# One dense block's gate matrix added up in DRAM by scattered adds instead of being built by matmuls

## The chip, the cores and the metric

The kernel runs on one core of one Trainium2 chip. The metric is the device time of one execution in microseconds (us). TensorE multiplies matrices, VectorE (DVE) and ScalarE (ACT) do elementwise work, GpSimd (POOL) does some of that and issues the DMAs whose addresses are data, SyncE (SP) issues most plain DMAs. Each engine works through its own list of instructions in order.

## The reference

One encoder layer over 512 tokens of width 1024: a mixer (two branches and a projection), then PEER, a product-key mixture of 128 x 128 single-neuron experts, and a final norm. The change touches PEER alone:

```python
def block(xb):                                  # 128 tokens at a time
    qh = (xb @ w_q).reshape(T, 8, 2, 128)       # 8 heads, 2 halves
    s = jnp.einsum('thpc,hpnc->thpn', qh, sk)   # against 128 sub-keys
    s1, i1 = lax.top_k(s[:, :, 0], 16); s2, i2 = lax.top_k(s[:, :, 1], 16)
    # the 16 best of the 256 sums s1 + s2; their experts are i1 * 128 + i2
    g = softmax(top_s)
    u = u_tab[experts]; v = v_tab[experts]
    act = gelu(einsum('td,thkd->thk', xb, u)) * g
    return einsum('thk,thkd->td', act, v)
```

So each token uses 8 x 16 = 128 (expert, gate) pairs. Two heads can choose the same expert; their gates then add up.

## The kernel before, in words

The mixer comes first (`hyena`, then `hgrn`, eight heads, each with five projections of the weights `w_in`). A projection is 24 matmuls of 512 columns: fp32 is split into a high and a low half, and three products are added up. Its weights come through `wraw` (3 buffers), issued on SP in the order of use. ACT makes the high half (`whi`), DVE the low half (`wlo`).

PEER cuts the tokens into four blocks of 128. Block 0 (`GTB`) is gathered: for each of its 128 choices one indirect DMA on POOL's queue fetches 128 rows of `u` or `v` (`grow`), and DVE does the dot products and sums. Blocks 1 to 3 (`DTB`) are dense. The experts are taken as 128 "rows" of 128. For one row, `act_row` multiplies its `u` by the 384 tokens (24 matmuls of 384 columns, `ps_a`), ACT applies gelu (`gact`), and two rows make a pair. `gated` multiplies a pair by the gates, `combine` multiplies by the row's `v` (18 matmuls of 512 columns into `acc`).

The gates for that stand in `Gd` in DRAM, expert by token. `gates_out` makes them for one block in 32 iterations of 4 tokens: DVE compares indices (`one`) and multiplies by the gates (`own`), ACT copies (`rows`), PE does four fp32 matmuls, each two instructions in the trace (`ps_g`), ACT copies the result (`Gs`), SP stores it.

The order of the work is this.
- `queries`: 16 score units `hp` (a projection by `w_q`, four small matmuls, then `top16` on DVE for each of the four blocks: five instructions over 128 scores). From `hp` 8 on, one step of `select` is run beside each. `select` turns the scores of four heads (a "part") into experts `eid` and gates; parts 0 of blocks 1 and 2 are done here (`EARLY`).
- `main`: the other four parts and `gates_out` of the three blocks. `weave` sets an `act_row` beside every `PER` of the costs that they yield. `2 * KEPT + RING - LEFT` = 27 rows are done before the loop; the rows of `KEPT` = 7 pairs go to DRAM, the others wait in a ring in SBUF. The low halves of these rows (`ul`) are DVE's.
- The loop `rows` over the 128 rows, with the rest of `act_row`, `gated`, `split_v` (load `vraw`, halves `vh` on ACT and `vl` on DVE) and `combine`. `gathered` is woven in, 2.25 steps a row: the two parts of block 0's `select`, 7 steps each, then 256 gathers. In the loop `ul` is POOL's, in its queue among the gathers.

An instruction stands in its engine's list where a scheduler puts it; SP's list is in order too, so a load that waits holds up all loads behind it. Pools are stacked: the space of a closed pool goes to the next one, whose first writer then waits for the last user.

## Time and profile before

| | before |
|---|---|
| three runs | 2130.71, 2137.34, 2142.05 us (median 2137.34) |
| profiled execution, time | 2140.67 us |
| profiled execution, span from the first to the last instruction | 2138.9 us |
| first `top16` / first matmul into `acc` / last one starts | 820.5 / 1175.1 / 2130.8 us |

The busy time of an engine is its share of the span, and matmul ends are modelled, so the distance from one matmul's start to the next is a better price than its duration. The granted clock is TensorE's, 1.00 being the higher of its two levels.

### The profile page before, as it was taken

Reading aid. Unit: us, or ns where it says so; the run is one execution under the profiler, and the core shown is the slowest. Engines: PE = TensorE matmul, PEld = TensorE weight load, DVE = VectorE, ACT = ScalarE, POOL = GpSimd, SP = SyncE. Lnnn points to the kernel's source line nnn. Section 1 sums busy time; section 2 is a strip of 40 time slices with the busy share of each in tenths; the row PEclk is TensorE's granted clock in tenths of the full one; section 3 lists DMA queues with packets and bytes.
Section 4 is the critical chain, followed back from the end, with each engine's and each line's share of the span. In section 5 each row is a group of like instructions: output and inputs, shape, how many; then the busy total and the mean of one; then the engine's idle time right before and its main releaser. Section 6 shows DMA issues by size and latency. Waiting matters only on the chain.

```text
span 2138.9 us, 29773 instructions
## 1 busy us (share of the span) xinstructions
PE 2061.9 (96%) x11109; PEld 1819.3 (85%) x11109; DVE 1697.0 (79%) x3073; ACT 962.4 (45%) x1382; POOL 617.1 (29%) x361
## 2 busy tenths in 40 slices
PE   7999999999999999989989999999999999999998
PEld 6888888888888898778889888899888888899987
DVE  6788765999997648999999787787777668778765
ACT  5555435666565623337776332332332323332333
POOL 0000000000000000000001566777776666677640
PEclk9999999999999999989999999999999999999999
DMA  6212222221222434124547988888898888889964
GB/s 194 82 50 65 70 69 100 62 70 60 70 63 75 137 130 139 50 72 173 202 161 245 312 287 299 309 325 309 285 324 281 301 303 313 306 292 333 316 217 158
DMA packets 153661, 406.89 MB, mean 190 GB/s; under 512 B 12425, under 2 KB 65419, under 8 KB 151852
## 3 DMA queue, kind: packets, MB, share of 16 engines
q1 hardware_dynamic: 109884, 255.59, 35.5%
q0 software_dynamic: 36864, 134.23, 17.2%
q10 hardware_dynamic: 6768, 15.17, 2.0%
q8 instruction: 87, 1.43, 0.3%
q14 instruction: 58, 0.48, 0.1%
HBM read 372.83 MB, written 32.11 MB: 189 GB/s over the span
## 4 chain that ended last, share of the span: by engine, by line
PE 56%; DVE 20%; DMA 9%; issue 7%; ACT 4%; POOL 3%; DVEq 0%; ACTq 0%; POOLq 0%; SPq 0%
PE ps_mm L97 7%; PE ps_mm L95 7%; PE ps_mm L94 7%; PE acc L973 5%; PE acc L974 4%; PE acc L972 4%; PE ps_a L94 4%; PE ps_a L97 4%; PE ps_a L95 4%; DMA grow<-in_u,gidx 3%; DMA vraw<-in_v 3%; DMA grow<-in_v,gidx 2%; PE ps_g L1228 2%; POOL grow L904 2%; PE ps_x L718 2%
## 5 line engine op out<-in xcount | busy, mean ns | idle before, releaser
L86 POOL TENSOR_TENSOR ul<-uraw,uh 128x1024 fp32r<-128x1024 f32 x100 | 257.6, 2576 | 634.2 <-DMA uraw<-in_uT 396.4
L85 ACT CAST vh<-vraw 128x1024 fp32r<-128x1024 f32 x128 | 134.7, 1053 | 597.5 <-DMA vraw<-in_v 525.0
L94 PE MATMUL ps_a<-pxh,uh 128*128 128x384 f32 x1008 | 343.9, 341 | 23.6 <-ACT gact L865 23.4
L95 PE MATMUL ps_a<-pxl,uh 128*128 128x384 f32 x1008 | 342.3, 340 | 0.0
L973 PE MATMUL acc<-vl,gh 128*128 128x512 f32 x768 | 300.7, 392 | 0.4 <-DVE vl L86 0.4
L974 PE MATMUL acc<-vh,gl 128*128 128x512 f32 x768 | 300.8, 392 | 0.0
L972 PE MATMUL acc<-vh,gh 128*128 128x512 f32 x768 | 298.8, 389 | 0.0
L933 DVE SCALAR_TENSOR_TENSOR xg<-grow,gw,xg 128x1024 f32<-128x1024 f32 x127 | 194.9, 1534 | 88.6 <-DMA grow<-in_v,gidx 87.5
L94 PE MATMUL ps_mm<-xh,whi 128*128 128x512 f32 (+1 forms) x656 | 259.4, 397 | 1.6 <-ACT xh L195 1.3
L924 DVE SCALAR_TENSOR_TENSOR grow<-grow,xg 128x1024 f32<-128x1024 f32 x128 | 189.4, 1497 | 88.5 <-DMA grow<-in_u,gidx 88.5
L95 PE MATMUL ps_mm<-xl,whi 128*128 128x512 f32 (+1 forms) x656 | 255.2, 390 | 0.3 <-DVE xl L196 0.3
L94 PEld LDWEIGHTS ps_a<-pxh,uh 128*128 128x128 f32 x1008 | 191.1, 190 | 34.1 <-ACT gact L865 30.8
L826 POOL IOTA iota<- 128x512 bf16 x1 | 1.2, 1237 | 756.5 <-DVE gt L281 756.5
L97 PE MATMUL ps_a<-pxh,ul 128*128 128x384 f32 x1008 | 200.9, 340 | 10.7 <-DVE ul L86 10.3
L86 DVE TENSOR_TENSOR vl<-vraw,vh 128x1024 fp32r<-128x1024 f32 x128 | 188.9, 1477 | 18.9 <-ACT vh L85 18.8
L904 POOL DMA_INDIRECT grow<-in_u,gidx x128 | 185.8, 1451 | 45.3 <-issue 22.4
L95 PEld LDWEIGHTS ps_a<-pxl,uh 128*128 128x128 f32 x1008 | 191.1, 190 | 3.2
L97 PEld LDWEIGHTS ps_a<-pxh,ul 128*128 128x128 f32 x1008 | 177.7, 190 | 12.9 <-DVE ul L86 12.3
L904 POOL DMA_INDIRECT grow<-in_v,gidx x128 | 172.3, 1346 | 34.8 <-issue 18.6
L85 ACT CAST whi<-wraw 128x1024 fp32r<-128x1024 f32 x112 | 117.3, 1050 | 133.1 <-PE ps_mm L95 122.6
L974 PEld LDWEIGHTS acc<-vh,gl 128*128 128x128 f32 x768 | 144.1, 188 | 30.2
L973 PEld LDWEIGHTS acc<-vl,gh 128*128 128x128 f32 x768 | 144.1, 188 | 28.9 <-DVE vl L86 0.8
(413 smaller groups left out, 4150.3 us busy)
## 6 DMA issues: line engine op xcount, KB each, us to landing
uraw<-in_uT SPq DMA_DIRECT2D x128, 512.0 KB, 6.9
vraw<-in_v SPq DMA_DIRECT2D x128, 512.0 KB, 5.5
wraw<-in_w_in SPq DMA_DIRECT2D x80, 512.0 KB, 3.6
Gd<-Gs SPq DMA_DIRECT2D x12, 2048.0 KB, 7.3
gt<-Gd SPq DMA_DIRECT2D x32, 768.0 KB, 9.4
wraw<-in_w_q SPq DMA_DIRECT2D x16, 512.0 KB, 4.3
wraw<-in_w_b SPq DMA_DIRECT2D x8, 512.0 KB, 3.6
wraw<-in_w_a SPq DMA_DIRECT2D x8, 512.0 KB, 4.3
```

The source lines that it names most:

```text
L85: nc.scalar.copy(hi, src)
L86: return (eng or nc.vector).tensor_sub(lo, src, hi).ins
L94: nc.tensor.matmul(out, ah, bh, start=(i == 0), stop=False)
L95: nc.tensor.matmul(out, *((al, bh) if late else (ah, bl)), start=False, stop=False)
L97: nc.tensor.matmul(out, *((ah, bl) if late else (al, bh)), start=False, stop=(stop and i == n - 1))
L718: nc.tensor.matmul(pl[:, cs], KM[:, 0, cs], KM[:, 1, cs], start=True, stop=True)
L904: nc.gpsimd.indirect_dma_start(out=t, out_offset=None, in_=tab, in_offset=bass.IndirectOffsetOnAxis(ap=gidx[:, j : j + 1], axis=0))
L924: nc.vector.scalar_tensor_tensor(t, t, 1.0, xg, op0=ALU.mult, op1=ALU.mult, accum_out=gdot[:, j : j + 1])
L933: nc.vector.scalar_tensor_tensor(gacc, t, gw[:, j : j + 1], gacc, op0=ALU.mult, op1=ALU.add)
L972: nc.tensor.matmul(acc[k][:, c], gh[:, ts_], vh[:, ds_], start=(r == 0), stop=False)
L973: nc.tensor.matmul(acc[k][:, c], gh[:, ts_], vl[:, ds_], start=False, stop=False)
L974: nc.tensor.matmul(acc[k][:, c], gl[:, ts_], vh[:, ds_], start=False, stop=(r == NK - 1))
```

## The change

Block 1 (`SCT`) no longer goes through `gates_out`. A DRAM array `Gx` of 128 x 128 x 128 floats is filled with zeros during the mixer (16 stores of 512 KB). As soon as a part of block 1 is selected, `add_gates` computes the places (expert x 128 + token) and issues 64 indirect DMAs on POOL's queue, one for each choice: each adds 128 floats, one a token, to 128 places. The 16 adds of a head wait for all 16 of the head before, since heads may share an expert. `gated` loads the gates of block 1 from `Gx` and of blocks 2 and 3 (`MTB`) from `Gd`, and multiplies twice.

Beside it: `KEPT` 13 for 7 and `RING` 14 for 16, so 37 rows stand ahead of the loop; an `act_row` beside each `hp` from 8 on, and two steps of `select`; the scores of block 0 are kept (`s0`), and its `top16` calls are put into `gathered`; `vraw` has three buffers; parts ahead of the gates count 1.3 times in `weave`.

```diff
-        C.Gd = dp.tile([12, P, P * 32], F32, name="Gd")
+        C.Gd = dp.tile([NG, P, P * GQ], F32, name="Gd")
+        C.Gx = {tb: dp.tile([P * P * P, 1], F32, name=f"Gx{tb}") for tb in SCT}
...
+        zero = mp.tile([P, 1024], F32, name="zero")
+        nc.vector.memset(zero, 0.0)
+        C.zeros = {tb: [] for tb in SCT}
+        for tb, gx in C.Gx.items():
+            dst = gx.rearrange("(p c x) o -> p c (x o)", p=P, x=1024)
+            for c in range(P * P // 1024):
+                C.zeros[tb].append(nc.sync.dma_start(dst[:, c], zero).ins)
...
+SCT = (1,)
+MTB = (2, 3)
 ND = len(DTB) * P
+NX = len(SCT) * P
 T0 = DTB[0] * P
-RING = 16
-KEPT = 7
+RING = 14
+KEPT = 13
+FIRSTC = 1.3
 LEFT = 3
 ...
 MIX = 3
-STEPS = 1
+STEPS = 2
 LAG = 4
 GQ = 32
-NG = ND // GQ
+NG = len(MTB) * P // GQ
...
+    row = cp.tile([P, 1], F32, name="row")
+    nc.gpsimd.iota(row, pattern=[[1, 1]], base=0, channel_multiplier=1, allow_small_or_imprecise_dtypes=True)
+    place = {tb: cp.tile([P, P], I32, name=f"place{tb}") for tb in SCT}
+    added = {}
+    def add_gates(tb, part):
+        n = HEADS // 2 * TOPK
+        ks = slice(part * n, part * n + n)
+        nc.vector.tensor_scalar(place[tb][:, ks], eid[:, tb, ks], float(P), row, op0=ALU.mult, op1=ALU.add)
+        for hd in range(part * HEADS // 2, (part + 1) * HEADS // 2):
+            ins = []
+            for j in range(hd * TOPK, hd * TOPK + TOPK):
+                i = nc.gpsimd.indirect_dma_start(out=C.Gx[tb], out_offset=bass.IndirectOffsetOnAxis(ap=place[tb][:, j : j + 1], axis=0),
+                                                 in_=gate[:, tb, j : j + 1], in_offset=None, compute_op=ALU.add).ins
+                tc.declare_no_dep(i, group=f"add{tb}.{hd}", reason="the experts of one head differ")
+                tc.add_to_no_dep_group(f"add{tb}.{hd}", i)
+                behind(i, added[tb, hd - 1] if hd else C.zeros[tb])
+                ins.append(i)
+            added[tb, hd] = ins
+    def behind(i, all_):
+        for o in all_:
+            tc.add_manual_dep(i, o.name, mybir.DependencyInfo(mybir.DependencyClass.Sync, mybir.DependencyReason.DATA), reason="sums in DRAM")
     gw = cp.tile([P, P], F32, name="gw")
     def chosen(pool, tb, part, ahead=2):
-        return select(C, pool, tb, part, v16, i16, gate, eid, pio, ahead)
+        yield from select(C, pool, tb, part, v16, i16, gate, eid, pio, ahead)
+        if tb in SCT:
+            add_gates(tb, part)
 
 ...
     puctx = ExitStack()
+    sgctx = ExitStack()
     pu = puctx.enter_context(tc.tile_pool(name="pu", bufs=UB, side="right"))
+    s0 = sgctx.enter_context(tc.tile_pool(name="sg", bufs=1, side="right")).tile([P, 16, P], F32, name="s0")
...
-    queries(C, xh, xl, v16, i16, chosen, fill)
+    queries(C, xh, xl, v16, i16, s0, chosen, fill)
     C.wctx.close()
 ...
         def main():
-            rest = [[chosen(sw, tb, part) for part in range(2) if part or k >= EARLY] for k, tb in enumerate(DTB)]
-            yield from chain(*rest[0])
-            for k, tb in enumerate(DTB):
-                nxt = chain(*rest[k + 1]) if k + 1 < len(DTB) else iter(())
+            rest = {tb: chain(*[chosen(sw, tb, part) for part in range(2) if part or k >= EARLY]) for k, tb in enumerate(DTB)}
+            for tb in SCT + MTB[:1]:
+                for c in rest[tb]:
+                    yield FIRSTC * c
+            for k, tb in enumerate(MTB):
+                nxt = rest[MTB[k + 1]] if k + 1 < len(MTB) else iter(())
...
-        yield from chosen(sw, GTB, 0, 1)
-        yield from chosen(sw, GTB, 1, 1)
+        for part in range(2):
+            for hp in range(part * HEADS, part * HEADS + HEADS):
+                top16(C, sw, v16[:, GTB, hp], i16[:, GTB, hp], s0[:, hp])
+                if hp % 2:
+                    yield 3.2
+            yield from chosen(sw, GTB, part, 1)
+        sgctx.close()
...
-        raw = pv.tile([P, D], F32, name="vraw")
+        raw = pv.tile([P, D], F32, name="vraw", bufs=3)
...
+            for b, tb in enumerate(SCT):
+                gx = pv.tile([P, GR, P], F32, name=f"gx{tb}")
+                ins = nc.sync.dma_start(gx, C.Gx[tb].rearrange("(r e t) o -> e r (t o)", e=P, t=P)[:, r : r + GR]).ins
+                behind(ins, added[tb, HEADS - 1])
+                prep["gx", b] = gx
...
-        g4 = g.rearrange("p r (g t) -> p r g t", t=GQ)
+        for b in range(len(SCT)):
+            nc.vector.tensor_mul(g[:, :, b * P : b * P + P], g[:, :, b * P : b * P + P], prep["gx", b][:, r % GR : r % GR + 2])
+        g4 = g[:, :, NX:].rearrange("p r (g t) -> p r g t", t=GQ)
...
-def queries(C, xh, xl, v16, i16, chosen, fill):
+def queries(C, xh, xl, v16, i16, s0, chosen, fill):
...
-            s = w2.tile([P, TB, P], F32, name="s")
-            nc.scalar.copy(s, pt.rearrange("p (t n) -> p t n", t=TB))
-            for tb in DTB + (GTB,):
-                top16(C, w2, v16[:, tb, hp], i16[:, tb, hp], s[:, tb])
+            pt = pt.rearrange("p (t n) -> p t n", t=TB)
+            s = w2.tile([P, len(DTB), P], F32, name="s")
+            nc.scalar.copy(s, pt[:, DTB[0] : DTB[-1] + 1])
+            nc.scalar.copy(s0[:, hp], pt[:, GTB])
+            for k, tb in enumerate(DTB):
+                top16(C, w2, v16[:, tb, hp], i16[:, tb, hp], s[:, k])
 
 ...
                 run(islice(early, STEPS))
+                next(fill)
```

SP's list in `hgrn`, at the end of the first head's five loads (the numbers tell buffers apart). Before, the second head's loads follow at once:

```order
L121 DMA wraw_3428<-in_w_in 128x1024
L121 DMA wraw_3460<-in_w_in 128x1024
L121 DMA wraw_3504<-in_w_in 128x1024
L121 DMA wraw_3569<-in_w_in 128x1024
L121 DMA wraw_3656<-in_w_in 128x1024
L121 DMA wraw_3716<-in_w_in 128x1024
```

and of the change:

```order
L121 DMA wraw_3479<-in_w_in 128x1024
L121 DMA wraw_3523<-in_w_in 128x1024
L594 DMA Gx1_69<-zero_3355 128x1024 x16
L121 DMA wraw_3588<-in_w_in 128x1024
L121 DMA wraw_3675<-in_w_in 128x1024
```

So the second head's loads (`wraw_3569` before, `wraw_3588` of the change) have moved behind all 16 stores. ACT's list at the same place, from the third weights' output to the second head's first weights; `sg` and `lf` (the forget gates) lie in the space that the pool of `zero` left. Before, with what each waits for:

```order
L603 COPY raw_3363<-ps_mm_3434 128x512 [waits PE_49]
L85 CAST whi_3571<-wraw_3569 128x1024 [waits DMAHW0_49,DVE_49,PE_49]
L603 COPY raw_3363<-ps_mm_3466 128x512 [waits PE_49]
L636 ACTIVATE so_3494<-raw_3363 128x1024 [waits Activation_49]
L110 ACT_TABLE_LOAD
L639 ACTIVATE lf_3495<-sg_3493,lbs_3335,omlb_3334 128x2x512
```

and of the change:

```order
L644 ACTIVATE so_3513<-raw_3382 128x1024 [waits Activation_49]
L110 ACT_TABLE_LOAD
L642 ACT_TABLE_LOAD [waits DMAHW4_49,DMAHW5_49,DMAHW3_49,DMAHW6_49,DMAHW2_49,DMAHW7_49,DMAHW1_49]
L642 ACTIVATE sg_3512<-raw_3382 128x1024 [waits DMAHW0_49]
L618 COPY vT_3554<-ps_mm_3529 128x512 [waits PE_49]
L647 ACT_TABLE_LOAD
L647 ACTIVATE lf_3514<-sg_3512,lbs_3336,omlb_3335 128x2x512 [waits Activation_49]
L627 COPY vh_3561<-ps_x_3556 128x512 [waits PE_49]
L85 CAST whi_3590<-wraw_3588 128x1024 [waits DMAHW0_49,DVE_49]
```

The activation into `sg` stood ahead of these rows; it has moved behind `so`, and its table load waits for the DMA queues of the stores (DMAHW). The cast of the second head's first weights (`whi_3571` before, `whi_3590` of the change) stood ahead of `so` and now stands behind it, six rows behind that wait.

SP's list at the loop's start, where the first gates are loaded. Before:

```order
L844 DMA uraw_11107<-in_uT 128x1024 [waits DMAHW6_49,DMAHW1_49,DVE_49]
L844 DMA uraw_11146<-in_uT 128x1024 [waits DMAHW7_49,DMAHW3_49,DVE_49]
L951 DMA gt_11088<-Gd_68 128x12x128 [waits DMAHW5_49,DMAHW2_49,PE_49]
L940 DMA vraw_11095<-in_v 128x1024
L940 DMA vraw_11101<-in_v 128x1024
L844 DMA uraw_11183<-in_uT 128x1024 [waits DMAHW4_49,Pool_49]
```

and of the change, where the load of `gx1` waits for POOL's eight DMA queues (DMASW, those of the adds), ahead of the first loads of `v`:

```order
L885 DMA uraw_11055<-in_uT 128x1024 [waits DMAHW5_49,DVE_49]
L885 DMA uraw_11109<-in_uT 128x1024 [waits DMAHW6_49,DMAHW2_49,DVE_49]
L1000 DMA gx1_11087<-Gx1_69 128x4x128 [waits DMASW5_49,DMASW4_49,DMASW6_49,DMASW3_49,DMASW7_49,DMASW2_49,DMAHW0_49,DMASW1_49,DMAHW4_49,DMASW0_49,PE_49]
L1004 DMA gt_11089<-Gd_68 128x8x128
L988 DMA vraw_11097<-in_v 128x1024
L988 DMA vraw_11103<-in_v 128x1024
L988 DMA vraw_11142<-in_v 128x1024 [waits DMAHW7_49]
```

## Rows read from the trace of the kernel before

**Rows 1.** The page, part 1: busy us, share of the span, instructions.

```profile
PE 2061.9 (96%) x11109; PEld 1819.3 (85%) x11109; DVE 1697.0 (79%) x3073; ACT 962.4 (45%) x1382; POOL 617.1 (29%) x361
```

**Rows 2.** Busy time by stretch: stretch, length, busy us (instructions), then PEclk, DMA share, GB/s.

```profile
820.00:915.00 95.00, 90.76 (x445) 73.89 (x444) 94.69 (x539) 29.12 (x41) 0.00 (x0) 0.99 0.22 67
915.00:960.00 45.00, 36.45 (x187) 34.94 (x185) 44.73 (x219) 18.07 (x22) 0.00 (x0) 0.86 0.22 77
960.00:1145.00 185.00, 171.69 (x1208) 161.38 (x1208) 182.48 (x439) 142.82 (x244) 0.00 (x0) 0.99 0.51 189
1145.00:1175.00 30.00, 26.10 (x142) 25.78 (x141) 29.90 (x89) 13.53 (x18) 10.21 (x4) 0.94 0.68 235
1300.00:2050.00 750.00, 738.31 (x3671) 663.85 (x3670) 573.41 (x513) 248.02 (x311) 515.35 (x301) 1.00 0.86 305
```

**Rows 3.** Waits of PE, 820 to 1175 us: first and last of five.

```profile
PE ps_a L97 <- DVE ul L86: 10.3, 4, 7.9
...
PE ps_g L1228 <- ACT rows L1220: 3.7, 7, 1.4
```

**Rows 4.** Timeline of PE: start us, us, engine, line, operation.

```profile
953.59 1.55 PE L97 MATMUL ps_a<-pxh,ul 128*128 128x384 f32 x8
954.97 0.33 PE L94 MATMUL ps_a<-pxh,uh 128*128 128x384 f32 x1
...
1108.86 2.04 PE L1228 MATMUL ps_g<-rows,own 128*128 128x128 f32 x16
1110.66 0.42 PE L94 MATMUL ps_a<-pxh,uh 128*128 128x384 f32 x1
```

**Rows 5.** Groups of PE's instructions, 820 to 1175 us: count, busy us, mean ns.

```profile
L1228 PE MATMUL ps_g<-rows,own 128*128 128x128 f32 x768 | 98.8, 281 | 9.2 <-DVE own L1221 5.3 <-ACT rows L1220 3.7
L94 PE MATMUL ps_a<-pxh,uh 128*128 128x384 f32 x232 | 81.3, 350 | 6.0 <-ACT gact L865 5.9
```

**Rows 6.** Timeline of DVE in `queries` and in `gates_out`.

```profile
849.07 0.48 DVE L1243 MAX8 v<-s 128x8 f32<-128x128 f32 x2
...
854.02 1.21 DVE L86 TENSOR_TENSOR wlo<-wraw,whi 128x1024 fp32r<-128x1024 f32 x1
...
1112.80 1.28 DVE L1221 TENSOR_TENSOR own<-one,tg 128x512 f32<-128x512 bf16 x2
1114.00 1.28 DVE L1218 TENSOR_TENSOR one<-iota,tr 128x1024 bf16<-128x1024 bf16 x2
```

**Rows 7.** `hgrn`'s first head: timelines of SP, ACT and PE.

```profile
325.86 11.21 SPq L121 DMA_DIRECT2D wraw<-in_w_in  x3
...
358.34 1.28 ACT L110 ACT_TABLE_LOAD   x1
359.64 1.25 ACT L639 ACTIVATE lf<-sg,lbs,omlb 128x1024 f32<-128x1024 f32 x1
...
360.07 1.98 PE L97 MATMUL ps_mm<-xh,wlo 128*128 128x512 f32 x8
```

**Rows 8.** DMA issues: count, KB each, median us from issue to landing.

```profile
Gd<-Gs SPq DMA_DIRECT2D x12, 2048.0 KB, 7.3
...
kept<-gact ACTq DMA_DIRECT2D x7, 384.0 KB, 2.7
```

**Rows 9.** Timeline of POOL in the loop.

```profile
1199.64 1.54 POOL L904 DMA_INDIRECT grow<-in_u,gidx  x1 [4.67 <-DVE gidx L912]
1201.49 1.55 POOL L904 DMA_INDIRECT grow<-in_u,gidx  x1 [0.30 <-issue]
...
1255.40 0.94 POOL L904 DMA_INDIRECT grow<-in_u,gidx  x1 [0.30 <-issue]
1256.64 0.93 POOL L904 DMA_INDIRECT grow<-in_u,gidx  x1 [0.31 <-issue]
```

**Rows 10.** Part 3 of the page: the gathers' queue; packets, MB, share of 16 engines.

```profile
q0 software_dynamic: 36864, 134.23, 17.2%
```

**Rows 11.** Waits, longest in total first, 1152 to 2139 us: total us, times, longest.

```profile
ACT vh L85 <- DMA vraw<-in_v: 525.0, 96, 16.7
...
DVE grow L924 <- DMA grow<-in_u,gidx: 88.5, 44, 7.9
```

## The prediction, made before the run

> **What bounds the kernel now.** I read the page first, then busy time by stretch, then the waits and timelines of the stretches that differ. PE is busy for 2061.9 of 2138.9 us [rows 1], and in the loop for 738.3 of 750 us [rows 2]: there is no quarter of the time to win from another engine. But a busy PE is not one at its pace. A 384-column matmul starts every 0.1725 us (8 in 953.59 to 954.97), a `ps_g` instruction every 0.1125 us (16 in 1108.86 to 1110.66) [rows 4], so a row of 24 takes 4.14 us; a projection takes 5.44 us, the distance at which SP issues its loads [rows 7]. From 820 to 1175 us PE does 14 projections (76.2), 120 instructions of scores (13.5), 768 `ps_g` (86.4) and 735 row matmuls (126.8; the three `ps_a` groups, of which one stands in [rows 5], and 40 in `ps_mm`): 303 us of work in 355. So 52 us are lost there. Five waits account for 29 of them [rows 3], and the clock fell to 0.86 of the higher level in the stretch 915 to 960 and 0.94 in 1145 to 1175, both of which hold gaps of PE [rows 2]. DVE is busy for 351.8 of the 355 us [rows 2]: from `queries` to the loop DVE sets the pace, and in the loop PE.
>
> **The change part by part.**
>
> *`gates_out` of block 1 goes.* PE loses 256 `ps_g` instructions (128 fp32 matmuls), 256 x 0.1125 = 29 us; the three transposes are nothing beside that. DVE loses 32 `one` and 32 `own`, which start 0.6 us apart when in a row (two in 1112.80 to 1114.00 [rows 6]): 38 us. ACT's copies go with it; ACT was not the bound.
>
> *Ten more rows ahead of the loop.* This moves 41 us of PE work out of the loop, and costs DVE 10 `ul` at the 1.21 us of the equally large `wlo` [rows 6], 12 us, which in the loop were POOL's.
>
> *`top16` of block 0.* Four take 4.95 us (849.07 to 854.02 [rows 6]), so 16 take 20 us. The scheduler leaves the first two instructions of most beside `queries`, so about 7 us stay and 13 us go into the loop's start.
>
> *Pre-loop sum.* I add up each engine in four stretches of the new order. In `queries` (14 projections, 14 us of scores, 10 rows) PE has 132 us, and DVE about 124 (48 `top16` 59, 24 low halves 29, two selections 28, 7 of block 0). A selection is 14 us: what is left of DVE's 351.8 us after `top16`, low halves, `one` and `own` and some 10 us of loop work, divided by seven. Then come ten rows without gates: PE 41 us, DVE 68 (four selections, ten `ul`); DVE gets a start of some 10 us in the last rows of `queries`, so PE loses about 16. Then 13 rows with the gates of blocks 2 and 3: PE 54 + 58 = 112, DVE 77 + 16 = 93. Then seven or eight rows to the first `acc`, balanced. PE's work to the first `acc` is 303 - 29 + 41 = 315 us. I take 28 us of loss, the 16 and 12 more for the seams (about a quarter of the 52 lost now): the first `acc` comes after 343 us instead of 355, with ten rows fewer behind it. In the whole that is 29 us of work and 24 of stalls, **-53 us**. The bounds of the stalls' -24: all but 10 of the seams' 12 go (-42), or the ten-row stretch gives back nearly what the rest wins (-5).
>
> *The zeros.* Eight MB are stored from SP's queue, behind the fifth load of the first head, which SP issues at 337 us (325.86 + 11.21 [rows 7]). A 2 MB store lands in 7.3 us, so 8 MB in 29; by the difference to 384 KB in 2.7 us [rows 8], in 23 and 2 of latency. They have landed at 361 to 369 us with the loads beside them; I take 366. Now the waits: ACT reaches the forget gates at 358.3 us [rows 7], and its table load for `sg` waits for all 16 stores. Behind it stand six rows (none over 1.28 us [rows 7]) and then the cast of the second head's first weights, so that PE can start on them some 7 us after the landing, at 373. Before, that cast had been done ahead, and PE went on at 362 (360.07 + 1.98 [rows 7]). The loads of the second head stand behind the stores too, but land before that. **+11 us** (6 to 14). DVE and PE are both nearly full in `hgrn`, so I give nothing back.
>
> *The adds.* 128 indirect DMAs on POOL, which had nothing to do before the loop. The trace has no accumulating DMA; the nearest are the gathers, with 128 rows as well. POOL issues one every 1.25 us while DVE is idle (1255.40 to 1256.64) and every 1.85 us while DVE is full (1199.64 to 1201.49) [rows 9]. Part 0 is selected when PE has done 9 projections, 11 scores and 2 or 3 rows, at 820 + 70 = 890 us (9 x 5.44 + 11 x 0.9 + 2.5 x 4.14; all clock times here are without the zeros' 11 us); part 1 at about 960. With 1.5 us in `queries`, 1.85 in `main`, and a landing of 3 us (384 KB take 2.7 [rows 8]) at each of eight heads, the adds end at 890 + 96 + 118 + 24 = 1128 us. They are needed when the first `gx` is issued, some 12 us ahead of the first `acc` (a load of up to 7 us as in [rows 8], the multiplications and halves): 820 + 343 - 12 = 1151. So they are **hidden, 0 us**, with 23 us to spare; at 1.25 us throughout there are 77, at 1.85 throughout it is 0. If that cover goes, every microsecond counts fully, since the loads of `v` stand behind `gx` in SP's list and the loop's `ul` behind the adds in POOL's.
>
> *The loop.* `gx` and the smaller `gt` carry the bytes of the old `gt`; `gkept` six pairs more. The multiplication is split in two (some 5 us of DVE in all). `vraw` with three buffers helps a little where ACT waits for `v` (525 us in total [rows 11]), though little of that reaches PE. I take 0 (-8 to +32; for the upper end see the second rival).
>
> *Sum.* -53 + 11 = -42 us. The span of the profiled execution becomes 2097 us, its time (1.8 us more than the span before) 2099. That execution lay 3.3 us above the median of the three runs, so the runs should have **2096 us**.
>
> **A rule against the change.** POOL's 0.94 us for an indirect DMA beside an idle DVE becomes 1.55 beside a full one [rows 9]. The Trainium skill, SBUF — State Buffer, section "SBUF: two separate sides", explains that DMAs issued from GpSimd have their descriptors written on GpSimd, which is shut out of a port that it shares with VectorE while VectorE runs certain operations; its section "A bandwidth-pool intuition that's wrong (but worth ruling out)" has a DMA of 620 ns grow to 3100 ns that way. By that 3.1 us, an estimate from the page, the adds would end 890 + 397 + 24 = 1311, 160 us late, and the kernel would need about 2256 us. By the row it is 1.85 us.
>
> **The rivals.**
>
> *The adds are late* (slower). An indirect DMA is 144 packets (36864 / 256), 9 an engine, of 17.2% x 16 x 2139 / 36864 = 160 ns [rows 10]. If a 4-byte packet costs an engine as much as one of 4 KB, that is 1.4 us an add, hidden by POOL's pace. If the sum in place costs two of them, it is 2.9 us an add: 890 + 371 + 24 = 1285, 134 us late, about 2230 us. From 2.3 us an add on the kernel is slower than before by half a per cent. For it: nothing shows what a read, add and write of 4 bytes costs. Against it: the engines work on eight adds at a time, and a small packet should not cost what 4 KB cost. The Trainium skill, DMA: Bandwidth & Descriptors, "Specifications", says that below 512 B an engine reads, modifies and writes anyway; that would speak for the doubled cost, and no run shows it yet.
>
> *The loop does not get shorter by the ten rows.* It moved 282 MB before (128 rows of `v`, 256 gathers, 100 of `u`, `gt`, `gkept`) and moves 279 after, in 41 us less; the rate in the middle of the loop is 305 GB/s at a DMA share of 0.86 [rows 2]. If that is the pace, bytes win back 9 us of the 41, and 32 are lost: about 2128 us. For it: DVE waited 88.5 us for the gathers of `u` alone [rows 11]. Against it: PE is busy for 98% there, so DMA does not set the pace yet, and the share would rise only to about 0.9.
>
> *Better than forecast.* The stalls shrink to the seams' 10 us and the zeros cost 6: about 2073 us.
>
> **How the numbers follow.** Half a per cent, 10.7 us, is about what a measurement here can tell from no change, so "same" is 2126.7 to 2148. Chances: forecast (2082 to 2112) 0.55; better 0.11; the longer loop (2112 to 2140) 0.19, two thirds of it faster by over half a per cent or near; adds late by up to 50 us 0.07, by more 0.08. Faster: 0.55 + 0.11 + 0.10 = 0.76; slower: 0.08 + a little of the mild lateness = 0.11; same 0.13. The range is 2070 to 2138.
>
> **What the profile of the changed kernel would show.** No `ps_g` of block 1; PE's loss from the first `top16` to the first `acc` near 28 us, most of it in the rows before the first `one`; a wait of ACT for the stores near 358 us, PE idle behind it for about 11; POOL's adds 1.25 to 1.85 us apart, the last landing 20 us before the first `gx`; loop rows of about 7.2 us. Wrong would make it: adds over 2 us apart or heads that take long to land (SP then waits at `gx`), PE gaps in the loop with DVE or ACT waiting for `grow` or `vraw`, or the ten-row stretch losing 30 us.

## The result, and the profile after

The changed kernel takes **2111.32 us** (median of 4 runs, 2109.67 to 2115.97) against 2134.95 for the kernel before beside it (4 runs): a ratio of 0.9885, 95% interval 0.9855 to 0.9915. It is faster by some 24 us (1.1%), where 2096 us was forecast: the kernel is 15 us slower than that. The times of four kernels below (18 pairs of rows; the changed order with 13 and with 18; the zeros' own tile) fall into two groups 25 to 40 us apart, and both are given there.

The page of the kernel after, its first part and the clock (to be read beside [rows 1]):

```profile
span 2107.9 us, 29356 instructions
PE 2020.8 (96%) x10850; PEld 1792.6 (85%) x10850; DVE 1684.8 (80%) x3081; ACT 950.5 (45%) x1337; POOL 856.7 (41%) x480
PEclk9999999999999999999999699999999999999999
```

PE is busy for 41 us less, the span is 31 us shorter. GpSimd, which had only the loop's work before, is busy for 857 us. The clock, at its higher level nearly throughout before, has a slice of 0.6: slices are 52.7 us, and that one is the 23rd, from 1159 us on.

Busy time by stretch, after, with the columns of [rows 2]; 825.0 is the first `top16` and 1211.7 the first `acc`. The line that stands alone is the loop of the kernel before, up to its last matmuls, to be held against the fourth:

```profile
825.00:1211.70 386.70, 333.33 (x1954) 312.75 (x1953) 316.18 (x1166) 186.74 (x295) 243.53 (x132) 0.92 0.53 137
1040.00:1160.00 120.00, 117.26 (x833) 116.37 (x831) 101.61 (x224) 82.45 (x141) 92.41 (x49) 1.00 0.72 215
1160.00:1190.00 30.00, 0.00 (x0) 0.00 (x0) 0.00 (x0) 0.00 (x0) 25.16 (x16) 0.50 0.22 0
1211.70:2100.00 888.30, 886.09 (x4393) 794.22 (x4391) 738.87 (x817) 316.43 (x384) 611.61 (x343) 1.00 0.87 311
1300.00:2050.00 750.00, 748.36 (x3731) 673.69 (x3730) 631.39 (x617) 266.99 (x313) 563.99 (x318) 1.00 0.91 327
```

```profile
1175.10:2131.00 955.90, 937.79 (x4634) 838.51 (x4633) 716.07 (x696) 316.51 (x405) 605.42 (x352) 1.00 0.83 294
```

The three stretches, against the same ones of before: to the first `top16` 825.0 us instead of 820.5 (+4.5, forecast +11); from there to the first `acc` 386.7 instead of 354.6 (+32, forecast -12); from there to the end 896.2 instead of 963.8 (-68, forecast -41). The sum is -31 instead of -42, so two large errors nearly cancel. One stands in the third row: for 30 us PE, VectorE and ScalarE do nothing, GpSimd alone works, and the granted clock is 0.50, the lower level. The other is in the loop: it is 68 us shorter, 41 of them for ten rows fewer. Of the other 26, 16 are idle time of PE that is gone (888.30 - 886.09 = 2.2 us after, 955.90 - 937.79 = 18.1 before). Ten lie in its busy time, which falls by 52 us where ten rows are worth 41; no run here shows why the same matmuls stand shorter.

What ended those waits, after, 1150 to 1215 us (total, times, longest):

```profile
ACT gh L85 <- DVE gact L1014: 49.3, 2, 42.7
DVE gact L1012 <- DMA gx<-Gx: 39.5, 1, 39.5
PE ps_a L94 <- ACT gact L906: 39.5, 1, 39.5
```

and SP's queue and GpSimd's instructions around it (start, duration, what; idle time before it in brackets):

```profile
1147.94 0.33 SPq L885 DMA_DIRECT2D uraw<-in_uT  x1
1189.70 0.38 SPq L1000 DMA_DIRECT2D gx<-Gx  x1
1190.68 1.52 SPq L988 DMA_DIRECT2D vraw<-in_v  x3
```

```profile
896.18 1.98 POOL L854 DMA_INDIRECT Gx<-gate,place  x1 [134.16 <-DVE place L850]
898.47 1.57 POOL L854 DMA_INDIRECT Gx<-gate,place  x1 [0.30 <-issue]
927.89 1.70 POOL L854 DMA_INDIRECT Gx<-gate,place  x1 [0.30 <-issue]
932.63 1.55 POOL L854 DMA_INDIRECT Gx<-gate,place  x1 [3.05 <-DMA Gx<-gate,place]
...
1110.71 1.55 POOL L854 DMA_INDIRECT Gx<-gate,place  x1 [0.30 <-issue]
1118.33 9.44 POOL L854 DMA_INDIRECT Gx<-gate,place  x1 [6.08 <-DMA Gx<-gate,place]
1128.07 1.55 POOL L854 DMA_INDIRECT Gx<-gate,place  x1 [0.30 <-issue]
...
1160.59 1.54 POOL L854 DMA_INDIRECT Gx<-gate,place  x1 [0.86 <-issue]
1162.43 1.55 POOL L854 DMA_INDIRECT Gx<-gate,place  x1 [0.30 <-issue]
1164.29 1.55 POOL L854 DMA_INDIRECT Gx<-gate,place  x1 [0.30 <-issue]
1186.56 1.55 POOL L854 DMA_INDIRECT Gx<-gate,place  x1 [0.30 <-issue]
```

Read upwards: SP issues nothing from 1147.94 to 1189.70, since its next transfer is `gx`, which waits for the last add; VectorE waits for `gx` with the first product, ScalarE with the cast of that product (42.7 us), PE for ScalarE's `gelu`, which would free a buffer of PSUM. The adds began at 896.2 us, about as forecast (890 plus the zeros' 4.5), and ended at 1188 instead of 1133 (1128 + 4.5). Even from 1160 to 1187, when nothing else runs, they start 1.85 us apart: 1.55 on GpSimd and 0.30 between.

### The profile page after: what moved, and what is told of

Read it like the earlier page. It is cut to its first block, busy times and chain, and to the rows that moved or that the text cites. A ratio compares the mean times of both kernels' runs of the same rounds, so it can differ in the third digit from the quotient of the medians.

```text
span 2107.9 us, 29356 instructions
## 1 busy us (share of the span) xinstructions
PE 2020.8 (96%) x10850; PEld 1792.6 (85%) x10850; DVE 1684.8 (80%) x3081; ACT 950.5 (45%) x1337; POOL 856.7 (41%) x480
## 3 DMA queue, kind: packets, MB, share of 16 engines
q0 software_dynamic: 55296, 134.31, 19.8%
## 4 chain that ended last, share of the span: by engine, by line
PE 72%; DVE 10%; POOL 6%; ACT 4%; issue 3%; DMA 3%; SPq 1%; DVEq 0%; ACTq 0%; POOLq 0%
PE ps_mm L95 8%; PE ps_mm L94 8%; PE ps_mm L97 8%; PE acc L1029 8%; PE acc L1028 8%; PE acc L1027 8%; PE ps_a L97 6%; PE ps_a L94 6%; PE ps_a L95 6%; POOL Gx L854 5%; PE ps_x L726 1%; PE ps_x L94 1%; PE ps_x L97 1%; PE ps_x L95 1%; DMA Gx<-gate,place 1%
## 5 line engine op out<-in xcount | busy, mean ns | idle before, releaser
L94 PE MATMUL ps_a<-pxh,uh 128*128 128x384 f32 x944 | 320.2, 339 | 44.4 <-ACT gact L906 44.4
L95 PE MATMUL ps_a<-pxl,uh 128*128 128x384 f32 x944 | 318.4, 337 | 0.0
L854 POOL DMA_INDIRECT Gx<-gate,place x128 | 230.0, 1797 | 196.1 <-DVE place L850 134.2
L86 POOL TENSOR_TENSOR ul<-uraw,uh 128x1024 fp32r<-128x1024 f32 x90 | 245.6, 2730 | 153.0 <-ACT uh L85 152.2
L94 PEld LDWEIGHTS ps_a<-pxh,uh 128*128 128x128 f32 x944 | 179.2, 190 | 49.5 <-ACT gact L906 46.2
L947 POOL DMA_INDIRECT grow<-in_u,gidx x128 | 197.4, 1542 | 42.2 <-issue 17.6
L947 POOL DMA_INDIRECT grow<-in_v,gidx x128 | 182.7, 1427 | 41.0 <-issue 19.7
L85 ACT CAST uh<-uraw 128x1024 fp32r<-128x1024 f32 x128 | 134.7, 1052 | 137.9 <-PE ps_a L95 90.7
L97 PE MATMUL ps_a<-pxh,ul 128*128 128x384 f32 x944 | 184.8, 336 | 0.3 <-POOL ul L86 0.3
L95 PEld LDWEIGHTS ps_a<-pxl,uh 128*128 128x128 f32 x944 | 179.3, 190 | 4.0
```

The costliest lines, as they stand in the source:

```text
L85: nc.scalar.copy(hi, src)
L86: return (eng or nc.vector).tensor_sub(lo, src, hi).ins
L94: nc.tensor.matmul(out, ah, bh, start=(i == 0), stop=False)
L95: nc.tensor.matmul(out, *((al, bh) if late else (ah, bl)), start=False, stop=False)
L97: nc.tensor.matmul(out, *((ah, bl) if late else (al, bh)), start=False, stop=(stop and i == n - 1))
L854: i = nc.gpsimd.indirect_dma_start(out=C.Gx[tb], out_offset=bass.IndirectOffsetOnAxis(ap=place[tb][:, j : j + 1], axis=0), in_=gate[:, tb, ...
```

## The experiments

**Half the adds.**

```
-            for j in range(hd * TOPK, hd * TOPK + TOPK):
+            for j in range(hd * TOPK, hd * TOPK + TOPK, 2):
```

> Every second add of each head is left out (64 of 128; the waits between heads stay), so block 1's gates are incomplete. The changed kernel's adds run from 896 to 1188 us without a break, and PE stands still from 1158 to 1198. Theory A (the adds are late, and all of it counts): the adds end near 1055, PE has no gap ahead of the first acc, which comes near 1170, and the time is 2111 - 40 = about 2070. Rival B (the gap only moves the loss: while PE stood still the loop's buffers were filled, and that is why the loop after it loses 2 us and not the 18 to 28 of the kernel before): the gap goes, the loop loses 20 to 28 again, about 2090 to 2098. Rival C (something else than the adds holds the first gx): the gap stays, 2111.

Measured: 2071.6 us (4 runs, 2067.1 to 2074.9), ratio 0.9689 (0.9659 to 0.9720). Its busy time from the first `top16` to the first `acc`, and PE's waits in the whole loop:

```profile
824.90:1172.60 347.70, 331.39 (x1954) 310.94 (x1953) 316.06 (x1166) 186.55 (x295) 129.61 (x68) 0.97 0.51 152
```

```profile
PE acc L1028 <- DVE vl L86: 0.9, 1, 0.9
PE ps_a L94 <- ACT gact L906: 0.7, 1, 0.7
```

Theory A holds to 2 us, rivals B and C fall: the gap is gone, the loop still loses under 2 us. So the adds' lateness costs 2111.3 - 2071.6 = 40 us, and the stretch without it takes 347.7 us, where the prediction had 343. The loop's gain has another cause.

**Two buffers of `v` again; and the three numbers alone.** The changed kernel without the third buffer (first diff and expectation), and two made from the kernel before, with PE adding up all the gates: three numbers of the change, the third buffer among them (second diff and expectation), and the same without the diff's last line (third expectation).

```
-        raw = pv.tile([P, D], F32, name="vraw", bufs=3)
+        raw = pv.tile([P, D], F32, name="vraw")
```

```
-RING = 16
-KEPT = 7
+RING = 14
+KEPT = 13
...
-        raw = pv.tile([P, D], F32, name="vraw")
+        raw = pv.tile([P, D], F32, name="vraw", bufs=3)
```

> Two buffers of v again instead of three. The changed kernel's loop loses 2 us of PE from the first acc on, the kernel before 18 to 28. Theory A (the loop gained by other means: ten rows fewer, or the gap ahead of it): about 2111 to 2116. Rival B (the third buffer is what won it): about 2131 to 2137, with ACT and PE waiting in the loop.

> The kernel before, with PE adding up all the gates as there, and three numbers of the change alone: 13 pairs of rows in DRAM, ring of 14, three buffers of v. No add, no zeros. Theory A (the 26 us that the changed kernel's loop lost less come from the third buffer, and the ten rows ahead of the loop cost there what they save in it): the loop loses 2 to 5 us of PE instead of 18 to 28, about 2110 to 2118, as fast as the changed kernel. Rival B (the third buffer only pays beside the adds or the gap): about 2137. Rival C (VectorE, which sets the pace ahead of the loop, pays 12 us for ten low halves, and the loop gains): 2120 to 2128.

> The kernel before with 13 pairs of rows in DRAM and a ring of 14 alone; v has two buffers. With the third buffer this kernel takes 2114. Theory A (the third buffer alone gave those 24 us): 2137 or more; the changed kernel lost 72 us when its third buffer went, so up to 2185 can be. Rival B (the rows gave it): 2114 to 2120.

Measured (behind the runs the ratio to the kernel before beside them, and its interval): 2183.6 us (6 runs, 1.0218, 1.0179 to 1.0257) for the changed kernel with two buffers; 2113.8 (6 runs, 0.9882, 0.9857 to 0.9907) for the three numbers alone; 2182.4 (4 runs, 1.0178, 1.0139 to 1.0217) for the two numbers. Waits in the loop with three buffers and then with two, both without adds:

```profile
ACT vh L85 <- DMA vraw<-in_v: 39.9, 13, 6.0
```

```profile
ACT vh L85 <- DMA vraw<-in_v: 517.7, 91, 17.7
POOL ul L86 <- ACT uh L85: 267.3, 40, 10.2
PE ps_a L94 <- ACT gact L865: 40.8, 13, 5.2
```

ScalarE waits 518 us for `v` with two buffers (as in [rows 11]) and 40 with three. SP issues loads in one order: where the next load of `v` waits for a buffer, the loads of `u` and `kept` behind it wait too, `uh` and `ul` come late, and PE waits with `ps_a` (40.8 us, and 10 more at `acc`). This chain is read from the order of the lists; SP's queue stands at loads of `v` for VectorE's `vl` with three buffers as well (564 us in all, against 630), and no run takes the links apart. The stretch up to the first `acc` hardly differs (1212.9 us with three buffers, 1215.7 with two); the loop does, 898 us against 974. PE's idle time accounts for 51 of these 75 us; the rest is in its busy time, at a granted clock of 0.97 instead of 1.00.

The third buffer is worth 72 us with the adds (2183.6 - 2111.3) and 69 without (63 by the two ratios). Rival B of the first expectation was right, and I had its size too small; of the other two, theory A held. More: the three numbers alone give what the whole change gives. Next to them the adds, the zeros and the search of block 0's keys in the loop come to nothing, 2111 against 2114. The two numbers without the buffer make the kernel before 1.8% slower, which I can't explain further. The buffer alone in the kernel before was not run, so how the 24 us split between it and the two numbers is not shown.

**Ten rows more ahead of the loop.**

```
-KEPT = 13
+KEPT = 18
```

> 18 pairs of rows in DRAM instead of 13, all adds kept: ten more rows of 4.14 us ahead of the loop, none of which needs the gates. Theory A (PE's gap of 39.5 us is only for want of rows): the rows fill the gap, the adds end at 1188 as before, the first acc stays near 1210, the loop has ten rows fewer: 2111 - 40 = about 2071. Rival B (the loop does not get shorter by its rows, as it moves 327 GB/s at a DMA share of 0.91 and five more pairs must be loaded again): 2090 to 2111. Rival C (more stores and loads while the adds run slow them down, and what waits for them moves back by as much): over 2080 with a first acc after 1225.

Measured: 2136.7 us (median of 12 runs: 5 of 2108, 7 of 2135 to 2142). The lower group wins 3 us against the change, not 40. In the profiled execution, one of the upper group (GpSimd first, then ScalarE):

```profile
1081.98 1.55 POOL L854 DMA_INDIRECT Gx<-gate,place  x1 [0.30 <-issue]
1091.99 35.46 POOL L854 DMA_INDIRECT Gx<-gate,place  x1 [8.46 <-DMA Gx<-gate,place]
1127.75 1.68 POOL L854 DMA_INDIRECT Gx<-gate,place  x1 [0.30 <-issue]
```

```profile
1157.86 1.04 ACT L85 CAST uh<-uraw 128x1024 fp32r<-128x1024 f32 x1
1230.83 1.04 ACT L85 CAST vh<-vraw 128x1024 fp32r<-128x1024 f32 x1 [71.93 <-DMA vraw<-in_v]
```

Only rival C's numbers came (over 2080; the first `acc` of this execution is at 1286.4), with another cause. The ten rows were not done in the gap: the cast of the first row of `v` stands ahead of them on ScalarE, its load stands behind `gx` on SP, and so ScalarE waits 71.9 us with 13 rows left to do. And one add, the first of a head, took 35.46 us, so that the adds ended at 1220 us. There is no profile of the lower group.

**The order at the loop's start.** `v` first, `gx` behind the last row, low halves of these rows on VectorE; with 18 and with 13 pairs.

```
-        act_row()
-        gated(0)
         for r in range(AHEAD):
             split_v(r)
-            if r:
-                act_row()
+            act_row()
+        looping.append(True)
+        gated(0)
         gated(1)
...
-    looping.append(True)
...
-                behind(ins, added[tb, HEADS - 1])
+                behind(ins, added[tb, HEADS - 1] + ([last_gelu[0]] if r == 0 else []))
```

> 18 pairs of rows in DRAM again, and the order at the loop's start changed so that nothing which waits for the adds stands ahead of the rows: the loads and casts of the first three rows of v come first, the first load of block 1's gates waits for the last row ahead of the loop as well as for the adds, and the low halves of these rows stay on VectorE (on GpSimd they stood behind the adds). All adds kept. Theory A (the kernel with 18 pairs won nothing since the cast of v, whose load stands behind the gates' load, shut ScalarE for 72 us with 13 rows left to do): those rows run from 1158 to 1212, the adds end near 1190, the first acc comes near 1215, the loop takes 843 to 850 us as there: about 2068. Rival B (the rows are not what the gap wants, the adds' end sets the loop's start with another 20 us behind it and the loop loses what the gap gave): 2090 to 2110. Rival C (an add stands for 35 us as in the kernel with 18 pairs, so that the gates come at 1222): first acc near 1235, about 2090.

> The same order at the loop's start with the 13 pairs of the changed kernel. Theory A (order and rows are both needed): PE runs out of rows near 1165, the gap shrinks from 39.5 to some 25 to 30 us, about 2097 to 2103. Rival B (order alone is enough, the gap goes): 2070. Rival C (rows alone count, order nothing): 2111.

Measured with 18 pairs: 2097.2 us (median of 6 runs: 2 of 2072 to 2073, 4 of 2097 to 2100), with 13: 2126.3 (4 runs: one of 2088, three of 2124 to 2130). The profile of a 2072 of the first has the first `acc` at 1216.2 and its longest add takes 14.24 us; that of a 2124 of the second has an add of 35.33. In the lower groups theory A holds with 18 pairs (2068 forecast): the order wins 36 us there (2108 to 2072). With 13 the one lower run is 23 us faster than the change, more than A said; the other three are slower than the change. The upper group with 18 pairs lies 7 us above what rival C gave for an add of 35 us (2090).

**The two groups.** In the two profiled executions of upper groups an add stood for 35 us, in those of the lower ones for 14 (9.44 in the changed kernel). VectorE, while the 35.46 lasted:

```profile
1089.49 1.29 DVE L1280 TENSOR_TENSOR own<-one,tg 128x512 f32<-128x512 bf16 x2
1090.70 1.29 DVE L1277 TENSOR_TENSOR one<-iota,tr 128x1024 bf16<-128x1024 bf16 x2
1091.90 1.28 DVE L1280 TENSOR_TENSOR own<-one,tg 128x512 f32<-128x512 bf16 x2
...
1125.35 0.67 DVE L1277 TENSOR_TENSOR one<-iota,tr 128x1024 bf16<-128x1024 bf16 x1
1126.18 1.23 DVE L86 TENSOR_TENSOR ul<-uraw,uh 128x1024 fp32r<-128x1024 f32 x1 [0.16 <-issue]
1127.32 0.69 DVE L1280 TENSOR_TENSOR own<-one,tg 128x512 f32<-128x512 bf16 x1
```

`one`, `own` and `ul` follow each other without a pause from 1083.5 to 1126.0, and each reads two operands from SBUF; the first pause (0.16 us) is at 1126.18, and the add ended at 1127.45. The changed kernel has the same stream, without a pause from 1082.10 to 1128.08. There the first add of that head was issued just ahead of it and that of the next head in its middle:

```profile
1081.63 1.55 POOL L854 DMA_INDIRECT Gx<-gate,place  x1 [2.16 <-DMA Gx<-gate,place]
1118.33 9.44 POOL L854 DMA_INDIRECT Gx<-gate,place  x1 [6.08 <-DMA Gx<-gate,place]
```

It is so in all six profiles of kernels with all the adds and with `own` from SBUF: the first add of a head that falls into this stream stands until the stream ends. In the two upper executions a head began early in the stream (1090.6 and 1092.0 us). In the four others one began up to 2.4 us ahead of it and got through (1.55 to 1.73 us), and the next in its middle (1113 to 1118 us). VectorE need not pause to let the add go: the 9.44 us ended at 1127.77, where it made no pause.

The Trainium skill, SBUF — State Buffer, section "Who interferes with whom", says that a VectorE instruction with two SBUF inputs contends with a GpSimd instruction that reads SBUF, and one with a single input outside certain modes doesn't. The Trainium skill, SBUF — State Buffer, says in the same section that `tensor_tensor`, which `one`, `own` and `ul` all are, did not stall a DMA in a probe, and infers that writing descriptors needs the write side of the shared ports. The 35.46 us here speak against that. To see whether the second operand in SBUF matters, `own` takes its gates from PSUM:

```
-    tg = gb.tile([P, P], F32, name="tg", bufs=2)
-    pt = ps_g.tile([P, 512], F32, name="ps_g")
+    pt = C.ps_t.tile([P, 512], F32, name="ps_t")
...
-    nc.scalar.copy(tg, pt[:, 2 * P : 3 * P])
+    tg = pt[:, 2 * P : 3 * P]
```

(`pt` in a bank of its own, `ps_t`), with 18 pairs and the changed order; beside it the same with the zeros stored from GpSimd's queue out of a tile of their own.

> The kernel with 18 pairs and the changed order, whose times fall into two groups (2072 and 2097), and one thing more: the gates that own is multiplied by are read from PSUM, so that own has one operand in SBUF instead of two, and takes as long. In the slow executions one add, the first after the wait for a head's landing, stands on GpSimd for some 35 us, as long as VectorE runs one, own and ul (each with two operands in SBUF) without a pause. Theory A (GpSimd gets at SBUF only when VectorE doesn't read two operands there): in the stretch of one and own no add takes over 3 us any more, the adds end by 1190 and all executions lie near 2070. Rival B (an add stands since its head's last write or its descriptors are late for a reason of the DMA queues): the two groups stay, and single adds of 9 to 35 us in that stretch with them.

> The same, and the zeros are stored from GpSimd's queue, which is idle then, out of a tile that nothing else uses. Theory A (the zeros' 4.5 us come from SP's queue, where the second head's weights are issued behind 16 stores): PE does not wait near 364 us, the first top16 starts near 820.5 and the time is 4 us less than that of the kernel beside it, about 2066. Rival B (the stores take the DMA engines from those loads, whoever issues them): 825 and 2070, as there.

Measured: 2074.5 us (5 runs, 2072.8 to 2075.6; 0.9687, 0.9657 to 0.9716), and 2065.7 (6 runs, 2063.5 to 2068.3; 0.9650, 0.9624 to 0.9677). GpSimd at the same seam (the place where one head's adds end and the next one's begin) with `own`'s gates read from PSUM, and at the one seam inside that stream in the second kernel:

```profile
1082.71 1.55 POOL L854 DMA_INDIRECT Gx<-gate,place  x1 [0.30 <-issue]
1092.66 1.88 POOL L854 DMA_INDIRECT Gx<-gate,place  x1 [8.40 <-DMA Gx<-gate,place]
1094.84 2.09 POOL L854 DMA_INDIRECT Gx<-gate,place  x1 [0.30 <-issue]
```

```profile
1115.74 1.92 POOL L854 DMA_INDIRECT Gx<-gate,place  x1 [4.04 <-DMA Gx<-gate,place]
```

The head ends and the next waits for its landing where they did in the kernel with 18 pairs (8.40 us instead of 8.46), and VectorE runs the same instructions just as long (0.68 us a single `own`); but the add after the seam takes 1.88 us, not 35.46, and none of the 128 over 3.28 (4.92 in the second kernel, after that stream). All executions lie in one group. That speaks for two SBUF operands in every instruction of the stream as a condition of the long stand.

Three things stay open. The add stood through more than 50 instructions of VectorE, while adds that follow one another inside a head got through the same stream in 1.55 to 2.04 us (1083 to 1112 us in the changed kernel). With `own`'s gates in PSUM these became slower, 2.04 us in the median instead of 1.55; theory A's bound of 3 us was just missed, and the adds ended at 1207.9 us where it had 1190, as they began 4.7 us later than with `own` from SBUF and the waits between heads came to 33 us instead of 24. And both kernels with PSUM ran on another chip than those with two groups, so the times alone don't exclude the chip as a cause; the adds at 1092.66 and 1115.74 us speak against it. That the executions of the upper groups which were not profiled have such an add too is inferred.

The second kernel is 8.8 us faster than the first, where 4 were forecast: its first `top16` starts at 820.5 us, as theory A said, that of the first at 829.2.

**The zeros in a tile of their own**, from SP's queue as in the change, with 13 pairs and the change's order:

```
-        zero = mp.tile([P, 1024], F32, name="zero")
+    zero = cp.tile([P, 256], F32, name="zero")
...
+            C.zeros[tb].append(nc.sync.dma_start(dst[:, c], zero[:, None].to_broadcast([P, 4, 256])).ins)
```

> The zeros are stored from a tile of 256 columns that nothing else uses afterwards (each store reads it four times), so that no instruction of the stage waits for the stores to end; all else as in the changed kernel. Theory A (the whole price of the zeros is the wait for the tile's place): the first top16 starts near 820.5 as in the kernel before, not 825.0; 2107. Rival B (the stores' traffic delays the loads beside them): the first top16 stays at 825, 2111. Neither moves the gap ahead of the first acc by more than these 4.5 us, since the adds start where top16 does.

Measured: 2112.0 us (12 runs: nine of 2101 to 2115, three of 2140 to 2143; 0.9871, 0.9852 to 0.9891, of the nine), first `top16` at 825.9. ScalarE no longer waits for the stores (3.3 us after the change), yet nothing is won. SP's queue with the zeros on it, and without (the kernel of 2065.7 us, which has them on GpSimd's queue):

```profile
335.50 21.19 SPq L594 DMA_DIRECT2D Gx<-zero  x16
356.79 14.73 SPq L121 DMA_DIRECT2D wraw<-in_w_in  x5
```

```profile
334.87 35.34 SPq L121 DMA_DIRECT2D wraw<-in_w_in  x6
```

With 16 stores on SP the next head's weights are issued from 356.8 on, the cast of the first starts at 366.4 us instead of 358.9, and PE is idle for 5.1 us from 360 to 400 instead of 1.3. With the stores on GpSimd's queue, at the same traffic (330 GB/s from 330 to 360 us, against 323), the loads are issued on time and the first `top16` starts at 820.5. Rival B's numbers came, but its cause, the traffic, falls: the price of the zeros is their place in SP's queue.

**Stores instead of adds.**

```
-                                                 in_=gate[:, tb, j : j + 1], in_offset=None, compute_op=ALU.add).ins
+                                                 in_=gate[:, tb, j : j + 1], in_offset=None).ins
```

> Each of the 128 indirect DMAs stores its gates instead of adding them (the sums of experts chosen by several heads are lost); all waits stay. In the changed kernel they are never less than 1.85 us apart, with VectorE idle too, while gathers of whole rows are 1.25 apart. Theory A (the sum makes an add dearer on GpSimd): 1.25 us apart where VectorE rests, the last near 1110 to 1130, PE's gap gone, about 2070. Theory B (what is dear is a store of 4 bytes to each of 128 places, sum or not): 1.85 apart, end near 1188, 2111.

One run, 2123 us. Duration of such an instruction (least, median, most, in ns):

```profile
L854 POOL DMA_INDIRECT Gx<-gate,place x128: 952/958/11052, 897.6 to 1135.4; - x128
```

The median is 0.96 us, against 1.55 with the sum, so adding costs 0.6 us on GpSimd and theory A holds for the pace. It isn't the number of packets: GpSimd's queue has 144 for an add, as for a gather, and 32 for a store (55296 and 40960 in all, 36864 of them the gathers'), and a gather with its 144 takes 0.94 us beside an idle VectorE [rows 9]. PE's gap ahead of the first `acc` is gone too, but the time isn't theory A's 2070: from 962 to 990 us VectorE had no instruction to run (27.6 us), PE for 21.6 in the same stretch, while GpSimd went on at its pace. The profile names nothing that they waited for, and with one run it stays open. The 11.05 us are a store in the stream of `one` and `own`, the second of its head; it ended at 1115.72 us, with the first two instructions of a single operand in that stretch (1114.80 and 1115.60).

**What the adds are worth.** The three numbers alone, with `KEPT = 18`.

> No adds, all the gates added up on PE as in the kernel before; three buffers of v, a ring of 14, and 18 pairs of rows in DRAM, as many as in the fastest kernel here (2066). It tells what the adds are worth once nothing stands behind them. Theory A (without the adds VectorE sets the pace ahead of the loop, and ten more rows there cost PE and VectorE what the loop saves): 2105 to 2116, so that the adds are worth 40 to 50 us. Rival B (rows were all that it wanted, PE's stalls ahead of the loop are filled by them): 2070 to 2090.

Measured: 2112.0 us (4 runs, 0.9852, 0.9823 to 0.9880). Without adds more rows ahead of the loop change nothing (first `acc` at 1253.6); with adds that hold little up as many rows give 2065.7. Theory A holds: the adds are worth up to 46 us, and in the change as made they gave none of it. The 2065.7 has the changed order, `own`'s gates in PSUM and the search of block 0's keys in the loop as well; none of these was run without the adds, so what part of the 46 us is theirs is not shown.

## Why the prediction was right, and where it was off

The sign and the range held, in part by luck: without the 26 us from a term forecast at 0 the kernel would have come out at 2137 us, no faster than before and at the very end of the range. The steps:

- **PE's 29 us and the stalls ahead of the loop**: right to 5 us. With half the adds, which no longer hold up the loop, the stretch takes 347.7 us (343 forecast).
- **The zeros**: 4.5 us instead of 11. The wait of ScalarE for the stores came, 3.3 us long, but without it the 4.5 us stayed; they go with the stores' place in SP's queue.
- **The adds are "hidden, 0 us, with 23 us to spare"**: this is the step that failed, and it cost 40 us. I took 1.5 us an add in `queries` from gathers that take 0.94 or 1.55 [rows 9]. An add takes 1.55 + 0.30 in any case, as the sum itself costs 0.6 us: 128 x 1.85 = 237 us where I had 214. Slow adds came to 32 us more (230.0 us busy less 128 x 1.545), the waits between heads to 23 (24 forecast). Together 292 instead of 238. That late adds then hold up everything behind `gx` was right. The first rival was this mechanism, with 2.3 us an add as the point from which the kernel is slower than before; it came to (292 - 23) / 128 = 2.1. The cause that it named, small packets on the DMA engines, is not what set the pace: GpSimd's 1.55 + 0.30 is. The 3.1 us an add that I weighed against the change are not the price of every add (median 1.55 us). A GpSimd held up by VectorE is what the one of 9.44 us shows; for the dozen adds of 2.4 to 3.3 us beside a busy VectorE it is likely and not shown.
- **The loop, "0"**: this term was mis-sized by 26 us. With two buffers of `v` the changed kernel loses them and more (2183.6 us), and the three numbers alone win as much in the loop. I had seen ScalarE's 525 us of waits [rows 11] and said that little of it reaches PE. The rival of a loop that doesn't get shorter by its ten rows is refuted: it takes 896 us instead of 964, at a DMA share of 0.91 in its middle.

In short: -42, and +44 in the middle, -26 in the loop and -6.5 for the zeros make -30.5; the spans differ by -31.0.

## What to carry to other kernels

A chain of small transfers that is "off the path" is on it as soon as an in-order queue holds its consumer: count what stands behind the first reader on each queue, and put everything that doesn't need the chain ahead of it. When an edit bundles several, run the plain numbers alone: here a third buffer and two constants gave as much as the whole change, and the new mechanism paid (up to 46 us more) only once its reader's place in the queues and its seams were mended.

## What the runs showed of the hardware

- An indirect DMA of 128 x 4 bytes takes 0.96 us on GpSimd as a store (one run) and 1.55 as a sum, with VectorE idle too, and 0.30 between two.
- The first add after a wait for the head before stood on GpSimd for 9 to 35 us, until the end of a stream of VectorE instructions with two SBUF operands; with one operand of `own`, about every other instruction, in PSUM it took 1.88 and 1.92 us, and the adds inside a head 2.04 in the median instead of 1.55.
- With 13 pairs of rows in DRAM, a third buffer at one load in a shared, in-order queue was worth 63 to 72 us.
- At the end of `hgrn`'s first head, 16 stores of 512 KB ahead of the next loads in SP's queue made the first `top16` 4 to 9 us later; from GpSimd's queue, at the same traffic, they cost nothing.
